# A half-rotary embedding on one core: the store of tile 1 waits for a subtraction instead of the multiplication ahead of it

## The chip, the cores and the metric

The kernel runs on one core of one Trainium2 chip. The metric is the device time of one execution in microseconds (us); lower is better. Of the kernel before three executions were timed, and one more was recorded by the hardware profiler.

## The reference

The input `x` has the shape (16, 512, 16, 64): batch, sequence, heads and the 64 elements of a head, in float32. `cos` and `sin` have the shape (512, 32), of which the first 16 columns are used. Cut to what matters:

```python
x1, x2 = x[..., :32], x[..., 32:]
c, s = cos[None, :, None, :16], sin[None, :, None, :16]
first  = x1[..., :16] * c - x1[..., 16:] * s
second = x1[..., :16] * s + x1[..., 16:] * c
out = concatenate([first, second, x2], axis=-1)
```

Half of each head is rotated and the other half is copied. 33.55 MB are read and as many are written.

## The kernel before, in words

**Tiles.** The input is cut into four tiles (0 to 3). A tile has 128 partitions with 16 sequence rows (`K = 16`) of 16 heads of 64 elements each, 64 KB in each partition and 8.4 MB in all. The tile `ring` in SBUF has three slots, and tile t lies in slot t mod 3. So tile 3 is loaded into the slot of tile 0, and that load has to wait until tile 0 has been stored. A slot holds its tile as it was loaded and is overwritten in place by the rotated half; a store writes the whole slot, both halves.

**Tables.** `cos` and `sin` are loaded once on GpSimd's queue (L64, L65), and VectorE spreads them over the 128 partitions (L74 to L84). This happens at the start and has no part in the change.

**The rotation.** All arithmetic is VectorE's, in the function `rotate`, which takes a tile and a range of its rows and issues four instructions: a multiplication by the sine into a scratch tile `b_t` in PSUM (L97), a multiplication by the cosine in place (L98), a subtraction on the first 16 columns (L99), and an addition on the next 16 (L106). `rotate` returns two things: one instruction, and the list `done` of its additions. The first of the two is used for one thing alone, the variable `near`, from the call for rows 0 to 4 of tile 2 (`KM = 5`).

**The order of the work.** The order on each queue is the order in which the program is written. VectorE rotates tile 0 (rows 0 to 7, then 8 to 15), tile 1 (likewise), tile 2 (rows 8 to 15, then 0 to 4, then 5 to 7), and tile 3 (rows 0 to 7, then 8 to 15). SyncE's queue issues the loads of tile 0, of tile 1 and of rows 8 to 15 of tile 2, the two halves of the store of tile 0, the load of rows 0 to 7 of tile 2, the load of tile 3, and the store of tile 3. GpSimd's queue issues the loads of the tables, the store of tile 1 and the store of tile 2.

**The hold.** Tile 1 is rotated long before its store is issued. The function `hold` makes a transfer wait for one more instruction, and the store of tile 1 (`behind_loads`) is held in this way until `near`; the reason that the code gives is that the store is to follow the loads at the DMA engines. Behind it on GpSimd's queue stands the store of tile 2, which waits for the last addition of tile 2.

Of the kernel before, what the change touches and what calls it, by code (L numbers as in the profile page):

```python
# [1 line left out]

# [4 lines left out]


@with_exitstack
def kernel(  # L10
    ctx: ExitStack,
    tc: tile.TileContext,
    x: bass.AP,
    cos: bass.AP,
    sin: bass.AP,
    out: bass.AP,
):
    nc = tc.nc
    fp32 = mybir.dt.float32
    P = 128  # L20
    B, S, H, D = x.shape
    Q = D // 4
    HF = D // 2

    K = 16
    T = B * S // (P * K)
    PB = S // K
    REP = P // PB  # L30
    R = H * D
    NS = 3
    KC = K // 2
    KM = 5
    KP = K - 4

    xf = x.rearrange("b s h d -> (b s h d)").rearrange("(t p f) -> t p f", t=T, p=P)
    of = out.rearrange("b s h d -> (b s h d)").rearrange("(t p f) -> t p f", t=T, p=P)
    cosf = cos.rearrange("(p k) j -> p (k j)", k=K)
    sinf = sin.rearrange("(p k) j -> p (k j)", k=K)  # L40

    const_pool = ctx.enter_context(tc.tile_pool(name="const", bufs=1))
    b_pool = ctx.enter_context(tc.tile_pool(name="bp", bufs=1, space=bass.MemoryType.PSUM))


    ring = const_pool.tile([P, NS, K, H, D], fp32)
    stage = const_pool.tile([P, 2, K, HF], fp32)
    spun = const_pool.tile([P, 2 * K, Q], fp32)
    packed = const_pool.tile([PB, 2 * K, Q], fp32)
    table = const_pool.tile([P, 2, K, 2, Q], fp32)  # L50

    def rows(t, lo, hi):
        return ring[:, t % NS, lo:hi].rearrange("p k h d -> p (k h d)")

    def load(t, lo=0, hi=K):
        return nc.sync.dma_start(out=rows(t, lo, hi), in_=xf[t, :, lo * R : hi * R])

    def store(t, lo=0, hi=K, queue=nc.sync):
        return queue.dma_start(out=of[t, :, lo * R : hi * R], in_=rows(t, lo, hi))  # L59


    nc.vector.memset(stage[:, :, :, 0:Q], 0.0)  # L62
    spread = stage.rearrange("(j b) t k i -> j b t (k i)", b=REP)
    nc.gpsimd.dma_start(out=spread[:, 0, 0], in_=cosf)  # L64
    nc.gpsimd.dma_start(out=spread[:, 0, 1], in_=sinf)  # L65
    load(0)
    load(1)
    load(2, KC, K)

    PQ = PB // REP
    nc.vector.stream_shuffle(  # L74
        out=spun[:],
        in_=stage.rearrange("p t k j -> p (t k) j")[:, :, 0:Q],
        mask=[j % PQ * REP for j in range(PB)],
    )
    for q in reversed(range(REP)):
        n = PQ * (q + 1)  # L80
        nc.vector.tensor_copy(out=packed[0:n], in_=spun[q * PB : q * PB + n])  # L81

    for r in range(REP):
        nc.vector.tensor_copy(  # L84
            out=table[r * PB : (r + 1) * PB].rearrange("p t k c j -> p (t k) c j"),
            in_=packed.unsqueeze(2).to_broadcast((PB, 2 * K, 2, Q)),
        )
    C = table[:, 0].rearrange("p k c j -> p k (c j)")
    Sn = table[:, 1].rearrange("p k c j -> p k (c j)")

    def rotate(t, lo, hi, cut=None):
        x1 = ring[:, t % NS, lo:hi, :, 0:HF]
        c = C[:, lo:hi].unsqueeze(2).to_broadcast((P, hi - lo, H, HF))
        s = Sn[:, lo:hi].unsqueeze(2).to_broadcast((P, hi - lo, H, HF))
        b_full = b_pool.tile([P, KC, H, HF], fp32, name="b_t")
        b_t = b_full[:, 0 : hi - lo]
        nc.vector.tensor_mul(out=b_t, in0=x1, in1=s)  # L97
        scaled = nc.vector.tensor_mul(out=x1, in0=x1, in1=c)  # L98
        nc.vector.tensor_sub(  # L99
            out=x1[:, :, :, 0:Q], in0=x1[:, :, :, 0:Q], in1=b_t[:, :, :, Q:HF]  # L100
        )
        ends = [hi - lo] if cut is None else [cut - lo, hi - lo]
        done = []
        for a, b in zip([0] + ends, ends):
            done.append(
                nc.vector.tensor_add(  # L106
                    out=x1[:, a:b, :, Q:HF],
                    in0=x1[:, a:b, :, Q:HF],
                    in1=b_t[:, a:b, :, 0:Q],
                )  # L110
            )
        return scaled, done

    def hold(transfer, point):
        tc.add_manual_dep(
            transfer.ins,
            point.ins.name,
            mybir.DependencyInfo(
                mybir.DependencyClass.Sync, mybir.DependencyReason.DATA
            ),  # L120
            reason="the store follows the loads at the DMA engines",
        )

    rotate(0, 0, KC)
    _, close = rotate(0, KC, K, cut=KP)
    hold(store(0, 0, KC), close[0])
    store(0, KC, K)
    load(2, 0, KC)
    load(3)
    rotate(1, 0, KC)  # L130
    rotate(1, KC, K)
    behind_loads = store(1, queue=nc.gpsimd)
    rotate(2, KC, K)
    near, _ = rotate(2, 0, KM)
    rotate(2, KM, KC)
    store(2, queue=nc.gpsimd)

    hold(behind_loads, near)
    rotate(3, 0, KC)
    rotate(3, KC, K)  # L140
    store(3)


# [1 line left out]
_INS = ['x', 'cos', 'sin']  # L145
_OUTS = [((16, 512, 16, 64), 'float32')]


# [23 lines left out]
```

## Time and profile before

| | us |
|---|---|
| median of three timed executions (161.75 to 162.19) | 161.84 |
| the profiled execution | 162.47 |
| its span, from the first to the last instruction | 160.7 |
| VectorE busy (70% of the span) | 113.0 |
| GpSimd busy (2% of the span) | 2.5 |

Data moved at 419 GB/s over the span, and 67.24 MB passed in all. TensorE and ScalarE do no work. The profile comes from one execution, and its times count from the first instruction. 1.8 us of the profiled execution lie outside its span, and that execution was 0.6 us longer than the median of the timed ones. "Issue" of a DMA is the instruction that starts it on a queue; the data move later, on the 16 DMA engines that all queues share. In a table by stretches of time, the DMA share counts each packet wholly in the stretch in which it begins, so that in a short stretch the share can be above 1.

### The profile page before, as it was taken

What the parts mean: (1) busy time and instruction counts of PE and PEld (TensorE: products, weight loads), DVE (VectorE), ACT (ScalarE), POOL (GpSimd) and SP (SyncE); (2) the same over time, 40 slices, a digit from 0 to 9 for tenths busy, and PEclk for the clock granted to TensorE, in tenths of its full rate; (3) what the DMA queues carried; (4) which work ended last, traced back from release to release, by engine and by line L of the source; (5) the groups of instructions that cost most, each with busy time, mean ns of one, the idle gap of its engine ahead of it and who ended that gap; (6) DMA issues with size and microseconds to landing.
All of it is one profiled execution on the core that took longest, in us unless ns stands there. A gap on an engine that the chain in (4) does not pass through costs nothing.

```text
span 160.7 us, 120 instructions
## 1 busy us (share of the span) xinstructions
DVE 113.0 (70%) x48; POOL 2.5 (2%) x8
## 2 busy tenths in 40 slices
DVE  1000959999999999999999999999999970000000
POOL 3000000000000000000000001010000000000000
DMA  7969969969899999999999699699799799799790
GB/s 261 522 277 538 490 294 522 490 294 522 375 408 392 473 432 400 465 441 400 408 506 522 277 506 490 294 490 506 310 490 506 310 490 473 343 490 473 343 490 33
DMA packets 1504, 67.24 MB, mean 419 GB/s; under 512 B 192, under 2 KB 192, under 8 KB 224
## 3 DMA queue, kind: packets, MB, share of 16 engines
q1 hardware_dynamic: 1152, 50.33, 73.1%
q0 software_dynamic: 352, 16.91, 24.3%
HBM read 33.69 MB, written 33.55 MB: 419 GB/s over the span
## 4 chain that ended last, share of the span: by engine, by line
DVE 62%; DMA 14%; issue 5%; DVEq 1%
DVE b_t L97 22%; DVE ring L98 22%; DMA ring<-in_x_dram 14%; DVE ring L106 10%; DVE ring L99 7%; DVEq L167 1%; DVEq L97 0%
## 5 line engine op out<-in xcount | busy, mean ns | idle before, releaser
L97 DVE TENSOR_TENSOR b_t<-ring,table 128x4096 f32<-128x4096 f32 (+2 forms) x9 | 35.6, 3959 | 2.1 <-DMA ring<-in_x_dram 1.9
L98 DVE TENSOR_TENSOR ring<-ring,table 128x4096 f32<-128x4096 f32 (+2 forms) x9 | 35.6, 3950 | 0.3
L99 DVE TENSOR_TENSOR ring<-ring,b_t 128x2048 f32<-128x2048 f32 (+2 forms) x9 | 18.4, 2050 | 0.3
L106 DVE TENSOR_TENSOR ring<-ring,b_t 128x2048 f32<-128x2048 f32 (+3 forms) x10 | 18.4, 1853 | 0.0
L74 DVE LOAD_MASK_SELECT spun<-stage x1 | 0.0, 14 | 14.6 <-DMA stage<-in_sin_dram 14.6
L84 DVE COPY table<-packed 32x1024 f32<-32x1024 f32 x4 | 2.7, 684 | 0.1
L59 POOL DMA_DIRECT2D out_dram<-ring x2 | 1.1, 550 | 101.4 <-DVE ring L98 93.6
L81 DVE COPY packed<-spun 32x512 f32<-32x512 f32 (+3 forms) x4 | 1.7, 416 | 0.1
L62 DVE MEMSET stage<- 128x512 f32 x1 | 0.5, 485 | 0.9 <-PEq L156 0.9
L74 DVE STREAM_SHUFFLE spun<-stage 128x512 f32<-128x512 f32 x1 | 0.7, 723 | 0.0
L64 POOL DMA_DIRECT2D stage<-in_cos_dram x1 | 0.6, 642 | 1.3 <-DVE stage L62 1.3
L65 POOL DMA_DIRECT2D stage<-in_sin_dram x1 | 0.5, 545 | 0.0
L156 POOL MEMSET const-float32-0.0<- 128x1 f32 x1 | 0.1, 98 | 0.2 <-issue 0.2
L156 POOL MEMSET const-bfloat16-1.0<- 128x1 bf16 x1 | 0.1, 101 | 0.0
L156 POOL MEMSET const-float32-1.0<- 128x1 f32 x1 | 0.1, 98 | 0.0
L156 POOL MEMSET const-uint8-127<- 128x1 uint8 x1 | 0.1, 98 | 0.0
## 6 DMA issues: line engine op xcount, KB each, us to landing
ring<-in_x_dram SPq DMA_DIRECT2D x2, 4096.0 KB, 40.7
out_dram<-ring SPq DMA_DIRECT2D x2, 4096.0 KB, 17.3
stage<-in_cos_dram POOLq DMA_DIRECT2D x1, 64.0 KB, 9.2
stage<-in_sin_dram POOLq DMA_DIRECT2D x1, 64.0 KB, 13.6
ring<-in_x_dram SPq DMA_DIRECT2D x3, 32.3
out_dram<-ring POOLq DMA_DIRECT2D x2, 33.7
out_dram<-ring SPq DMA_DIRECT2D x1, 28.2
```

What stands on the lines that cost most here:

```text
L59: return queue.dma_start(out=of[t, :, lo * R : hi * R], in_=rows(t, lo, hi))
L62: nc.vector.memset(stage[:, :, :, 0:Q], 0.0)
L64: nc.gpsimd.dma_start(out=spread[:, 0, 0], in_=cosf)
L65: nc.gpsimd.dma_start(out=spread[:, 0, 1], in_=sinf)
L74: nc.vector.stream_shuffle(out=spun[:], in_=stage.rearrange("p t k j -> p (t k) j")[:, :, 0:Q], mask=[j % PQ * REP for j in range(PB)],)
L81: nc.vector.tensor_copy(out=packed[0:n], in_=spun[q * PB : q * PB + n])
L84: nc.vector.tensor_copy(out=table[r * PB : (r + 1) * PB].rearrange("p t k c j -> p (t k) c j"), in_=packed.unsqueeze(2).to_broadcast((PB, ...
L97: nc.vector.tensor_mul(out=b_t, in0=x1, in1=s)
L98: scaled = nc.vector.tensor_mul(out=x1, in0=x1, in1=c)
L99: nc.vector.tensor_sub(out=x1[:, :, :, 0:Q], in0=x1[:, :, :, 0:Q], in1=b_t[:, :, :, Q:HF])
L106: nc.vector.tensor_add(out=x1[:, a:b, :, Q:HF], in0=x1[:, a:b, :, Q:HF], in1=b_t[:, a:b, :, 0:Q],)
L167: with _tile.TileContext(nc) as tc:
```

## The change

`rotate` returns its subtraction (L99) in place of its second multiplication (L98). Since only `near` uses that value, one thing follows: the store of tile 1 on GpSimd's queue waits for the subtraction of rows 0 to 4 of tile 2 instead of the multiplication ahead of it. No instruction is added or taken away, and the order on every engine and queue is the same.

```diff
         nc.vector.tensor_mul(out=b_t, in0=x1, in1=s)
-        scaled = nc.vector.tensor_mul(out=x1, in0=x1, in1=c)
-        nc.vector.tensor_sub(
+        nc.vector.tensor_mul(out=x1, in0=x1, in1=c)
+        first = nc.vector.tensor_sub(
             out=x1[:, :, :, 0:Q], in0=x1[:, :, :, 0:Q], in1=b_t[:, :, :, Q:HF]
         )
...
-        return scaled, done
+        return first, done
```

## The prediction, made before the changed kernel had run

> **What bounds the kernel now.** I first read the page's line of DMA shares and the chain that ended last.
>
> ```profile
> DVE  1000959999999999999999999999999970000000
> DMA  7969969969899999999999699699799799799790
> ...
> DVE 62%; DMA 14%; issue 5%; DVEq 1%
> ```
>
> The chain names VectorE (DVE) for 62% of the span. But VectorE is done at 131.5 us and the transfers go on for almost 28 us more, while the DMA row is full from the first slices to the last. The dips to 6 and 7 are an artefact of counting: a packet belongs to the slice in which it begins. So I take the 16 DMA engines as the bound: 67.24 MB at 419 GB/s are 160.5 us, the whole span. A change counts here only if it makes DMA engines idle or slow.
>
> Next, the timeline around the held store (POOL is GpSimd).
>
> ```profile
> 93.41 2.82 DVE L98 TENSOR_TENSOR ring<-ring,table 128x2560 f32<-128x2560 f32 x1
> 96.27 1.49 DVE L99 TENSOR_TENSOR ring<-ring,b_t 128x1280 f32<-128x1280 f32 x1
> 96.53 0.56 POOL L59 DMA_DIRECT2D out_dram<-ring  x1 [93.64 <-DVE ring L98]
> 97.67 1.48 DVE L106 TENSOR_TENSOR ring<-ring,b_t 128x1280 f32<-128x1280 f32 x1
> 99.19 1.77 DVE L97 TENSOR_TENSOR b_t<-ring,table 128x1536 f32<-128x1536 f32 x1
> ...
> 104.89 0.54 POOL L59 DMA_DIRECT2D out_dram<-ring  x1 [7.80 <-DVE ring L106]
> ```
>
> Columns: start, duration, instruction. The multiplication ends at about 96.24, and GpSimd issues the store of tile 1 at 96.53, 0.29 us later. The subtraction ends at 96.27 + 1.49 = 97.76.
>
> Last, the busy time by stretches. I laid each so that every one of the 16 engines begins exactly one data packet in it; share times width is then the mean duration of a packet.
>
> ```profile
> core 0: us, DVE busy (x) POOL busy (x), PEclk, DMA share, GB/s
> 1.70:2.60 0.90, 0.00 (x0) 0.90 (x2) 1.00 3.44 1165
> 4.70:5.60 0.90, 0.00 (x0) 0.00 (x0) 1.00 2.69 1165
> ...
> 49.85:50.65 0.80, 0.77 (x2) 0.00 (x0) 1.00 1.52 655
> 94.70:95.60 0.90, 0.90 (x1) 0.00 (x0) 1.00 2.69 1165
> 97.10:98.00 0.90, 0.90 (x2) 0.00 (x0) 1.00 3.05 1165
> ```
>
> A 64 KB packet takes 2.69 x 0.90 = 2.42 us in steady state (94.70). The last packets of the load of tile 3, which begin at 97.10 to 98.00, take 3.05 x 0.90 = 2.74 us: the hand-over to the store of tile 1 costs an engine 0.32 us on average. The first packets of the program (1.70), begun on cold engines, take 3.44 x 0.90 = 3.10 us, 0.68 too many. The hand-over from loads to the first store on SyncE's queue (49.85, packets of 32 KB) takes 1.52 x 0.80 = 1.22 us, against 1.21 in steady state, so next to nothing.
>
> The trace's records of single packets give the rest. The last load packets begin at 97.19 to 97.89 on the 16 engines and would end at 99.61 to 100.31 at the steady 2.42 us. They end at 99.84 to 101.46, and the store's first packets follow at once. From there to the end every engine has a packet, so what one loses here it ends late by. The engine that ends last (159.42) is the one that lost most, 1.15 us. It is also the only one that took a store packet before the load's closing signal.
>
> **The change, part by part.**
>
> 1. The trigger moves from the end of the multiplication to the end of the subtraction. The issue comes at 97.76 + 0.29 = about 98.04 instead of 96.53: 1.5 us later. One instruction of 1.49 us by its own row; nothing on VectorE is added. In the built program the subtraction raises a signal of its own and GpSimd's wait counts to it (before, it shared the addition's signal, at 99.16).
>
> 2. What stands behind it on GpSimd's queue is the store of tile 2, which waits until 104.61. GpSimd is free again at 98.04 + 0.56 = 98.60, so this costs nothing. Nobody on VectorE or SyncE waits for the store of tile 1 before the end: its slot isn't used again. SyncE's queue passes nothing new.
>
> 3. The later store at the DMA engines is the open point. At its own pace the first engine needs the store at 99.61, the last at 100.31. How long after the issue is a store ready for the engines? The lower bound is the first load of the program on SyncE's queue: issue at 0.74, first packet at 1.75, so 1.01 us. That makes 99.05, before any engine is free: no loss. On the last engine the store stood ready when its load packet began, at 97.89 (it went ahead of the signal), and on those that began up to 97.63 it did not: 1.1 to 1.4 us, by which 98.04 becomes 99.1 to 99.4, again early enough. The upper bound is what happened before: issue 96.53, first store packet 99.84, 3.31 us. That makes 101.35, and the engines would idle up to 1.5 us, the whole shift.
>
> 4. Ready is not yet hidden. An engine chooses its next packet about one packet ahead: the store of tile 3, issued at 131.51, was passed over by an engine that began a new packet at 134.60 and taken by one that did at 135.03, 3.1 to 3.5 us after its issue, against 1.01 on idle engines. The lead, from ready to the end of the last load packet, was about 2 us before. It becomes 0.2 to 1.2 us. The hand-over at 49.85 had a lead of 1.0 to 1.7 us (ready at 49.07 + 1.01, packets ending at 51.11 to 51.79) and cost nothing, so a lead of 1.0 is enough on that queue; most engines will have less. A cold start costs 0.68 by the row at 1.70, and no lead at all up to 1.5 by point 3. I take 0.6 us beyond today's loss, nearest to the cold start, and keep 0 and 1.5 as ends. Below nothing is possible too; see the second rival.
>
> 5. The pages bear on point 3. A row: GpSimd's issue at 96.53 under the subtraction took 0.56 us, the one at 104.89 under a multiplication with two operands in SBUF took 0.54, so VectorE didn't hold up GpSimd. The Trainium skill, SBUF — State Buffer, section "SBUF: two separate sides", says that GpSimd, which writes the descriptors of its own DMAs, is locked out by a VectorE instruction in a two-port mode until that ends. By that rule descriptors not written by 99.19, when the next multiplication begins, would wait until it ends at 100.96, and the change would cost about 1.4 us, as an estimate; no run here shows such a lock, and the two rows speak against it.
>
> The sum, on the profiled execution: span 160.7 + 0.6 = 161.3, with the 1.8 us outside it 163.1. That execution was 0.63 above the median, so against the median 161.84 + 0.6 = 162.45.
>
> **The rivals.**
>
> Nothing changes: the store is ready at 99.1 to 99.4, every engine finds it when its load packet ends, and the hand-over loses what it did. For it: points 1 to 3 taken with the 1.1 to 1.4 us, and that the latest engine, which sets the end, keeps the longest lead, 0.9 to 1.2 us. Against it: the hand-over at 97 already lost 0.32 where SyncE's at 50 lost nothing, so GpSimd's queue is less smooth than the 1.01 says. Time: 161.85, within 0.45.
>
> Faster: the stretched packets are the price of the store coming up while load packets are under way. Before, it comes up as those packets begin, and they lose 0.32 on average and 1.15 on the engine that ends last. If it comes up only in their last 0.2 to 1.2 us, or if the load's closing signal goes first everywhere, that engine gets its loss back. The most is 1.15, less what the others lose: those end by 159.18, 158.75 and 158.31, so if the two worst are cured the end comes 0.67 earlier, and with the third 1.1. The median execution had 0.6 us less to cure than the profiled one, so I price it at 0.75: 161.1. It decides if the cost depends on the overlap and if the lead of 0.2 to 1.2 us is enough.
>
> The wait is not the one the change says: were the subtraction still to share the addition's signal, the store would come at 99.45, 2.9 us later, the engines would idle at least 0.1 us by the 1.01 and up to 2.9, and the time would be near 163.3. The built program speaks against it; it is in the chance of slower.
>
> **How the numbers follow.** 0.3%, about 0.5 us, is what a measurement of this kernel can tell from no change. Slower by the short lead: 0.40, at 162.45; its own range is 162.35 to 163.3 (161.84 + 0.5 to 1.5). Unchanged: 0.28. Faster: 0.32, from 160.7 to 161.35. No case holds half, so the range must take in most of all three: from 160.95, which leaves out about a third of the faster case, to 163.1, which leaves out the upper part of the slower one.
>
> **What would show it.** In the changed trace the wait on GpSimd names L99, and the issue is at about 98.0. The stretch of the last load packets, opened at 97.10, shows the mean packet: above 2.74 us, or store packets that begin after a gap or take more than 2.42, if I am right; 2.74 if nothing changes; near 2.42, with the load landing by 100.7 on all engines, if the faster rival is. All transfers should end 0.6 us later than at 159.42, with VectorE unchanged. I am wrong if the packets run on without loss though the issue is at 98.0: then the lead doesn't matter.

## The result and the profile after

| | before | after |
|---|---|---|
| median of 13 timed executions, us | 162.19 (161.62 to 162.59) | 162.57 (162.39 to 162.92) |
| profiled execution, us | 162.47 | 162.59 |
| its span, us | 160.7 | 160.7 |
| last transfer ends, us (packet records) | 159.42 | 159.48 |

The ratio of after to before is 1.0026 (95% interval 1.0014 to 1.0039): a loss of 0.26%, or 0.4 us, just inside the 0.3% of the prediction. The kernel before was timed again beside the changed one; over 13 executions its median is 162.19, above the 161.84 of the three shown at first. The times after lie closer together than those before: they span 0.53 us against 0.97.

The wait moved as the change says. These are the waits on GpSimd and the timeline of the changed kernel:

```profile
POOL out_dram L59 <- DVE ring L99: 94.9, 1, 94.9
POOL out_dram L59 <- DVE ring L106: 6.3, 1, 6.3
```

```profile
95.97 1.49 DVE L99 TENSOR_TENSOR ring<-ring,b_t 128x1280 f32<-128x1280 f32 x1
97.37 1.48 DVE L106 TENSOR_TENSOR ring<-ring,b_t 128x1280 f32<-128x1280 f32 x1
97.75 0.56 POOL L59 DMA_DIRECT2D out_dram<-ring  x1 [94.86 <-DVE ring L99]
```

The issue comes 0.29 us after the subtraction's end (95.97 + 1.49). In this execution all of VectorE's work lies 0.3 us earlier than in the profile of before, so the issue shows at 97.75 and not at 98.04. The store of tile 2 waits 6.3 us instead of 7.8 behind it, and is issued as before when tile 2 is done.

The busy time by stretches of the changed kernel. The DMA share is the column before the GB/s, and a packet counts where it begins. In the stretches at 97.10, 99.60 and 103.40 each of the 16 DMA engines begins one data packet:

```profile
core 0: us, DVE busy (x) POOL busy (x), PEclk, DMA share, GB/s
...
97.10:98.00 0.90, 0.90 (x2) 0.24 (x1) 1.00 2.69 1165
99.60:100.20 0.60, 0.60 (x1) 0.00 (x0) 1.00 6.29 1748
102.00:103.30 1.30, 1.26 (x2) 0.00 (x0) 1.00 0.00 0
103.40:104.00 0.60, 0.60 (x2) 0.00 (x0) 1.00 4.03 1748
```

And the first packets of the store of tile 1 in the kernel before, 1.47 x 1.70 = 2.50 us:

```profile
99.80:101.50 1.70, 1.67 (x2) 0.00 (x0) 1.00 1.47 617
```

In the stretch at 102.00 none of the 16 engines begins anything. The last load packets (97.10) take 2.69 x 0.90 = 2.42 us, the steady duration: their stretch, 2.74 before, is gone. But the first packets of the store of tile 1 (99.60) take 6.29 x 0.60 = 3.77 us in place of 2.42, and the second ones (103.40) are again at 4.03 x 0.60 = 2.42. So the hand-over from loads to stores, which lost 0.39 us per engine before (0.32 in load packets and 0.07 in the store's), now loses 1.35, all in the store's first packets.

That the time rose by 0.4 us only, while the mean loss rose by 0.96, is a matter of which engine ends last. Before, the engine that ended last lost 1.15 us, one that was well ahead of it 1.61, and the others 0 to 0.75; after, all lose 1.2 to 1.5. The mean of the 16 engines' ends went from 158.22 to 159.18, the last from 159.42 to 159.48.

### The profile page after: what moved, and what is told of

Same layout as the page of the kernel before. It is cut to its first block, busy times and chain, and to the rows that moved or that the text cites. A ratio compares the mean times of both kernels' runs of the same rounds, so it can differ in the third digit from the quotient of the medians.

```text
span 160.7 us, 120 instructions
## 1 busy us (share of the span) xinstructions
DVE 113.0 (70%) x48; POOL 2.5 (2%) x8
## 4 chain that ended last, share of the span: by engine, by line
DVE 61%; DMA 14%; issue 5%; DVEq 1%
DVE b_t L97 22%; DVE ring L98 22%; DMA ring<-in_x_dram 14%; DVE ring L106 10%; DVE ring L99 7%; DVEq L167 1%; DVEq L97 0%
## 5 line engine op out<-in xcount | busy, mean ns | idle before, releaser
L98 DVE TENSOR_TENSOR ring<-ring,table 128x4096 f32<-128x4096 f32 (+2 forms) x9 | 35.6, 3950 | 0.3
L99 DVE TENSOR_TENSOR ring<-ring,b_t 128x2048 f32<-128x2048 f32 (+2 forms) x9 | 18.4, 2049 | 0.3
L59 POOL DMA_DIRECT2D out_dram<-ring x2 | 1.1, 552 | 101.1 <-DVE ring L99 94.9
```

The lines of the kernel that those rows point to most:

```text
L99: first = nc.vector.tensor_sub(out=x1[:, :, :, 0:Q], in0=x1[:, :, :, 0:Q], in1=b_t[:, :, :, Q:HF])
```

## The experiments

All edits are against the changed kernel unless another is named. Whether a store is "ready" no record shows; the text takes it to be ready as long after its issue as the first packet came on engines that had nothing to do: 1.13 to 1.28 us on GpSimd's queue (e2) and 0.85 to 0.96 on SyncE's (e8). "Loss" is what the trace's packet records show per engine at the hand-over, against 2.42 us a packet and no pause, as a mean over the 16 engines. Ratios are to the kernel before, timed alongside (median 162.24 for the first four, 162.17 for the next four).

| run | queue, wait | issue | loss, and where | last transfer ends | median, ratio (95%) |
|---|---|---|---|---|---|
| e1 | GpSimd, first multiplication | 93.50 | 0.64, load packets | 159.21 | 162.22, 1.0003 (0.9989 to 1.0018) |
| before | GpSimd, second multiplication | 96.53 | 0.39, mostly load packets | 159.42 | |
| e9, before again | GpSimd, second multiplication | 96.30 | 0.59, load packets | 159.21 | one time, 162.28 |
| after | GpSimd, subtraction | 97.75 | 1.35, store packets | 159.48 | 162.57, 1.0026 (1.0014 to 1.0039) |
| e10, after again | GpSimd, subtraction | 98.09 | 1.37, store packets | 159.64 | one time, 162.75 |
| e6 | GpSimd, multiplication of rows 0 to 6 | 98.47 | 1.18, store packets | 159.44 | 162.57, 1.0023 (1.0013 to 1.0033) |
| e2 | GpSimd, addition | 99.28 | 0.62, pause | 158.76 | 161.85, 0.9976 (0.9966 to 0.9987) |
| e4 | SyncE, its data alone | 76.94 | 0.55, load packets | 158.98 | 162.45, 1.0004 (0.9991 to 1.0017) |
| e7 | SyncE, second multiplication | 96.03 | 0.65, load packets | 158.78 | 162.34, 1.0012 (0.9998 to 1.0026) |
| e3 | SyncE, subtraction | 97.62 | 0.01 | 158.24 | 161.60, 0.9960 (0.9945 to 0.9976) |
| e8 | SyncE, addition | 98.98 | 0.06, pause | 158.19 | 161.66, 0.9961 (0.9947 to 0.9975) |
| e5 | ScalarE, subtraction | 97.71 | 0.79, store packets | 159.19 | 162.29, 1.0001 (0.9986 to 1.0015) |
| e12 | ScalarE, addition | 98.98 | 0.24, pause and store packets | 158.82 | one time, 162.08 |
| e11 | GpSimd, subtraction, row 0 stored early | 97.95 | 0.04, load packets | 159.00 | one time, 162.07 |

### First round: when and where the store is issued

The changed trace suggested Theory A: from 97.75 to the true start of data (103.5 less 2.42, so 101.1) are 3.35 us, the delay that the upper bound of the prediction had named. Theory B was a fixed price of the turn.

e1:

```diff
-        nc.vector.tensor_mul(out=b_t, in0=x1, in1=s)
+        first = nc.vector.tensor_mul(out=b_t, in0=x1, in1=s)
...
-        first = nc.vector.tensor_sub(
+        nc.vector.tensor_sub(
```

> The store of tile 1 waits for the sine multiplication of rows 0 to 4 (L97), which ends at 93.38 us, so its issue on GpSimd's queue comes at 93.4 to 93.7, 2.8 us earlier than before the change. Theory A (GpSimd's queue needs about 3.35 us from the issue to the first data, and an engine that runs out of load packets earlier than that stands idle): data at 96.8 to 97.0, ahead of the last load packets, so no packet is stretched by more than 0.1 us on average, some engines take a store packet before their last load packet, and the time is 1.0 us below that of before: ratio 0.994 (0.992 to 0.996). Theory B (turning from loads to a store of GpSimd's queue costs an engine 0.3 to 1.4 us each time, whenever it is issued): the stretch stays, on other packets, mean at least 0.3 us, and the time is within 0.3% of before.

Measured: no gain. The stretches of e1 that hold the load packets in flight when the store came up, and the two rounds of packets behind them:

```profile
94.80:95.70 0.90, 0.90 (x1) 0.00 (x0) 1.00 3.40 1165
97.60:98.90 1.30, 1.30 (x1) 0.00 (x0) 1.00 1.86 807
100.05:101.30 1.25, 1.22 (x2) 0.00 (x0) 1.00 1.93 839
```

3.40 x 0.90 = 3.06 us: the load packets ahead of the first store packet are stretched by 0.64, as Theory B has it. Then the engines take store, load and store packets in turn, and each round is at 1.86 x 1.30 = 2.42 and 1.93 x 1.25 = 2.41 us. So in this overlap only the first turn costs, and not the alternation of loads and stores.

e2:

```diff
-    near, _ = rotate(2, 0, KM)
+    _, ends = rotate(2, 0, KM)
+    near = ends[0]
```

> The store waits for the addition of rows 0 to 4, which ends about 1.4 us after the subtraction, so the issue comes at 99.1 to 99.4. Theory A (3.35 us from issue to data, engines idle until then): the first store packets end at about 99.15 + 3.35 + 2.42 = 104.9, 1.4 us later than in the changed kernel on every engine, and the time rises by the whole 1.4 us: 164.0, ratio to before 1.011 (1.009 to 1.013). Theory B (a fixed cost of a cold start of 1.2 to 1.5 us, the store being ready 1.1 to 1.4 us after its issue): the engines are free at 99.6 to 100.1 and the store is ready at 100.2 to 100.5, so only about 0.4 us is added: 162.95, ratio 1.005.

Measured: faster than both kernels, against either theory. Timeline and stretches of e2:

```profile
99.01 1.77 DVE L97 TENSOR_TENSOR b_t<-ring,table 128x1536 f32<-128x1536 f32 x1
99.28 0.56 POOL L59 DMA_DIRECT2D out_dram<-ring  x1 [96.39 <-DVE ring L106]
```

```profile
99.60:100.40 0.80, 0.80 (x1) 0.24 (x1) 1.00 0.01 0
100.40:100.60 0.20, 0.20 (x1) 0.00 (x0) 1.00 12.31 5243
```

The engines run dry and nothing begins until 100.40 (the 0.01 are closing signals); then all 16 begin within 0.2 us, 100.41 to 100.56 by the records, with packets of 12.31 x 0.20 = 2.46 us. That is 1.13 to 1.28 us after the issue, not 3.35: Theory A is out, and so is a cold start of 0.7 us or more after such a pause. Issued 1.5 us later than in the changed kernel, the store ends its first packets earlier (102.9 to 103.0 against 103.4 to 103.9). The mean loss, 0.62, is above that of the kernel before, but the pause is longest for the engine that was free first (at least 0.78, from 99.63 to 100.41) and shortest for the last (at most 0.28, from 100.29): it levels the engines, and the ends lie at 158.64 to 158.76.

e3:

```diff
-    behind_loads = store(1, queue=nc.gpsimd)
+    behind_loads = store(1)
```

> The store of tile 1 waits for the same subtraction as in the changed kernel, but is issued on SyncE's queue, behind the load of tile 3. Theory A (the 3.35 us belong to GpSimd's queue; SyncE's needs about 1.0): issue at 97.8 to 98.1, ready at 98.8 to 99.1, before any engine is free at 99.6; stretch at the hand-over at most 0.1 us on average, time 1.0 us below that of before: ratio 0.994 (0.992 to 0.997). Theory B (a lead of less than 1 us leaves the engines cold on any queue): first store packets stretched by 0.7 us or more, time like the changed kernel's, ratio 1.000 to 1.003.

Measured: no loss, as Theory A foresaw for another reason; the gain is 0.4% rather than 0.6%. Theory B's fixed price doesn't hold on this queue. The issue in e3, and its stretches, last load packets and first store packets:

```profile
97.62 0.34 SPq L59 DMA_DIRECT2D out_dram<-ring  x1
```

```profile
97.20:97.85 0.65, 0.65 (x2) 0.00 (x0) 1.00 3.73 1613
99.60:100.35 0.75, 0.75 (x1) 0.00 (x0) 1.00 3.24 1398
```

3.73 x 0.65 = 2.42 and 3.24 x 0.75 = 2.43 us. This is the fastest of the versions, level with e8.

e4, the same with the hold taken out:

```diff
-    behind_loads = store(1, queue=nc.gpsimd)
+    behind_loads = store(1)
...
-    hold(behind_loads, near)
```

> The store of tile 1 is issued on SyncE's queue behind the load of tile 3 and held for nothing but its own data (done at 77.1); being in the same queue it follows the load at the engines anyway. Both theories: no stretch at the hand-over, all engines full to the end, time 1.0 to 1.2 us below that of before: ratio 0.993 (0.991 to 0.996). If instead the hand-over is stretched here too, by 0.3 us or more, the cost belongs to the turn from loads to stores at this point of the program and neither theory holds.

Measured: a miss for both. The last load packets, which end before the store in the same queue begins, are stretched to 4.94 x 0.60 = 2.96 us:

```profile
97.25:97.85 0.60, 0.60 (x2) 0.00 (x0) 1.00 4.94 1748
```

So by the last sentence of the expectation neither theory held. A store that stands ready early costs about 0.6 us in the load packet ahead of it (0.55 here, 0.64 in e1), on either queue.

### Second round: queue and time of arrival apart

e5 and e6:

```diff
-    behind_loads = store(1, queue=nc.gpsimd)
+    behind_loads = store(1, queue=nc.scalar)
```

> The first four runs felled both theories: the store held till the addition (issue 99.28) put data on the engines 1.13 to 1.28 us after its issue, earlier than in the changed kernel, and lost only the idle gap (0.62 us per engine on average), while the changed kernel's first store packets are stretched by 1.35 us on every engine; on SyncE's queue with the same wait nothing was lost. Here the store waits for the subtraction and is issued on ScalarE's queue, a second queue like GpSimd's but started in the way of SyncE's. Theory C (taking the turn from one queue to another while the last load packet is under way costs about 1.3 us): the first store packets are stretched by 1.0 us or more, time like the changed kernel's, ratio to before 1.001 to 1.004. Theory D (the cost comes with GpSimd's queue alone): hand-over loss at most 0.2 us per engine, time like that of SyncE's queue with this wait, ratio 0.996 (0.994 to 0.998).

e6, against the kernel before:

```diff
-    KM = 5
+    KM = 7
```

> The kernel before with KM = 7: the store waits for the cosine multiplication again, but that of rows 0 to 6, which ends at about 98.1. The issue on GpSimd's queue falls at 98.35, between that of the changed kernel (97.75) and that of the wait for the addition (99.28), and the store is ready at 99.5 to 99.65 by the 1.13 to 1.28 us of the latter, 0 to 0.6 us before the engines come free (99.6 to 100.1). Theory C and D alike leave open where the cost ends. If it is paid by any store that comes up before an engine has run out of load packets: stretch of 1.0 us or more on most engines, data from 101 on, ratio 1.002 to 1.005. If it falls with the time that the store overlaps the last load packet: loss of at most 0.4 us per engine, the best of the waits on GpSimd's queue, ratio 0.995 to 0.998.

Measured, the first store packets of e5, then of e6:

```profile
99.60:100.60 1.00, 1.00 (x1) 0.00 (x0) 1.00 3.21 1049
```

```profile
99.65:100.15 0.50, 0.50 (x2) 0.00 (x0) 1.00 7.17 2097
```

ScalarE's queue gives 3.21 us, 0.79 too many, between the two theories: more than SyncE's queue with the same wait, less than GpSimd's. In e6 the mean is 7.17 x 0.50 = 3.59. It is not one value: 14 engines took the store straight behind the load's signal and needed 3.48 to 3.97, while the two that had paused, by 0.07 to 0.24 us, needed 2.72 and 2.81. Those two were through at 102.7 and 102.9, their neighbours at 103.2 to 103.9. So on GpSimd's queue the price is paid in the first store packet even when the store comes up only shortly before the engine is dry, and most of it falls away once the engine has paused.

e7, against the kernel before, and e8, against e2:

```diff
-    behind_loads = store(1, queue=nc.gpsimd)
+    behind_loads = store(1)
```

> The store waits for the cosine multiplication of rows 0 to 4 as before the change, on SyncE's queue. Issue at 96.2, ready 1.0 us later at 97.2, when the engines begin their last load packets (97.2 to 97.9). With the subtraction's wait (ready 98.6) nothing was lost on this queue, with no hold at all (ready long ago) 0.55 us in the last load packets. Theory E (an engine that knows its next packet, a store, when it begins the last load packet pays 0.2 to 1.0 us in that packet): loss between, 0.2 to 0.6 us per engine, mostly on engines that began after 97.2, ratio 0.997 to 1.000. If the queue alone matters and not the time: as with the subtraction's wait, loss under 0.1, ratio 0.996.

> The store waits for the addition, on SyncE's queue. Issue at 99.1, ready 1.0 us later at 100.1 to 100.15; the engines are free at 99.6 to 100.1, so that they idle 0.3 us on average and the latest of them not at all; the packets after the gap are no longer than 2.47 us. Loss 0.2 to 0.5 us per engine on average, ratio to before 0.997 to 0.999, between that of the subtraction's wait on this queue (0.996) and that of the addition's wait on GpSimd's (0.9976) or near them. A loss above 0.8 us would say that SyncE's queue too has a bad time of arrival and that GpSimd's is not special.

Measured: e7's last load packets take 6.14 x 0.50 = 3.07 us, a loss of 0.65, just above what Theory E allowed; all engines pay, and the ratio is a little above its range. In e8 the loss is 0.06, below what I expected, since the store was ready 0.85 to 0.96 us after its issue rather than 1.0 or later. Last load packets of e7, first store packets of e8 (4.09 x 0.60 = 2.45 us):

```profile
97.30:97.80 0.50, 0.50 (x2) 0.00 (x0) 1.00 6.14 2097
```

```profile
99.70:100.30 0.60, 0.60 (x1) 0.00 (x0) 1.00 4.09 1748
```

### Third round: the two kernels again, and two looks at the cause

> The kernel before, unchanged, profiled a second time. Its times spread over 161.6 to 162.6, the changed kernel's over 162.4 to 162.9. If the spread comes from the hand-over, the loss there differs from that of the first profile (0.39 us per engine on average, 1.15 on the engine that ended last), while all other stretches of the DMA engines lose the same; the hand-over's mean stays at 0.2 to 0.7, below the changed kernel's 1.35, and the last transfers end at 158.3 to 159.4.

> The changed kernel, unchanged, profiled a second time. The loss in the first store packets is there again on every engine, 1.2 to 1.5 us, with unstretched load packets ahead of it, and the last transfers end within 0.2 us of 159.5. If the 1.35 us were an accident of one execution, the loss would be nearer to that of the kernel before, 0.4.

Both kernels unchanged. Last load packets of the kernel before (3.35 x 0.90 = 3.02 us), and first store packets of the changed one (4.47 x 0.85 = 3.80 us):

```profile
97.10:98.00 0.90, 0.90 (x2) 0.00 (x0) 1.00 3.35 1165
```

```profile
99.50:100.35 0.85, 0.85 (x1) 0.00 (x0) 1.00 4.47 1234
```

The stretch after is no accident. The kernel before has a loss that varies: 0.39 and 0.59 on average, and 1.15 and 1.14 in the worst load packet. Between this pair of profiles the last transfer moves by 0.43 us, between the first pair by 0.06; the medians say 0.38.

One part of e9's expectation fails: the other stretches do not all lose the same. At the first turn from loads to a store, on SyncE's queue at about 50 us, a packet takes 1.19 x 1.10 = 1.31 us in e9, against 1.22 in the first profile of the kernel before:

```profile
49.60:50.70 1.10, 1.07 (x2) 0.00 (x0) 1.00 1.19 477
```

Over all the profiles this turn costs 0 to 0.2 us per engine, most in e7 (1.41 us a packet), though no edit touches the work up to there.

e11:

```diff
-    behind_loads = store(1, queue=nc.gpsimd)
+    store(1, 0, 1, queue=nc.gpsimd)
+    behind_loads = store(1, 1, K, queue=nc.gpsimd)
```

> The changed kernel with row 0 of tile 1 stored on GpSimd's queue as soon as it is rotated (issue at about 64), and the other 15 rows as the change has it. Theory F (GpSimd's queue is cold after 80 us without work, and its first packet pays): the queue has worked until about 75, so the hand-over at 99.6 loses at most 0.4 us per engine. Theory G (turning from loads to a store of another queue is what costs, if the engine has no pause): the first packets of the 15 rows (60 KB, steady 2.27 us) are stretched by 1.1 to 1.5 us as in the changed kernel.

Measured: a loss of 0.04, within Theory F's bound and against Theory G's 1.1 to 1.5. Its last load packets and the first packets of the 15 rows, 2.24 x 1.10 = 2.46 and 1.90 x 1.20 = 2.28 us:

```profile
98.60:99.70 1.10, 1.07 (x2) 0.00 (x0) 1.00 2.24 953
101.10:102.30 1.20, 1.20 (x1) 0.00 (x0) 1.00 1.90 819
```

But the row stored early pushed the loads back, so that they ended at 101.2 to 102.3 and not at 99.6 to 100.1, and the store, issued at 97.95, was ready at 99.1 to 99.2, 2 to 3 us ahead of the engines instead of 0.6 to 1.2. It must be compared with the kernel before, which with such a lead lost 0.39 and 0.59. That leans to Theory F, and doesn't settle it.

The traces of e3, e4, e5 and e7 speak against Theory F in its plain form. In these runs the store of tile 2 is GpSimd's first DMA since the tables, whose data were through by 13.1 us. It is issued at about 104.7, when the engines are taking store packets from another queue. In e4 every engine begins its first packet of that store in the second of these stretches:

```profile
107.20:108.30 1.10, 1.10 (x1) 0.00 (x0) 1.00 2.20 953
109.60:110.70 1.10, 1.10 (x1) 0.00 (x0) 1.00 2.20 953
```

2.20 x 1.10 = 2.42 us, the steady duration, ahead of the turn and in it; in all four runs no packet that begins from 103 to 114 takes longer. So neither a queue that has been without work for over 90 us nor a change of queue costs anything by itself. If either matters at 99.6, it does so together with the turn from loads to a store.

e12 (one time, 162.08, beside 162.33 for the kernel before), against e2:

```diff
-    behind_loads = store(1, queue=nc.gpsimd)
+    behind_loads = store(1, queue=nc.scalar)
```

> The store waits for the addition, on ScalarE's queue. Issue at 99.0 to 99.1; ready 1.0 us later, after most engines have run out of load packets. Theory G (only an engine that goes straight from a load packet to a store of another queue pays; one that has paused doesn't): engines with a pause lose the pause alone, first packets at most 2.5 us, mean loss below 0.5 us, against 0.78 with the subtraction's wait on the same queue, and any engine without a pause shows a first packet of 3.0 us or more. If a second queue always costs: 0.8 us in the first packets whether they pause or not.

Measured, the first store packets:

```profile
99.60:100.35 0.75, 0.75 (x1) 0.00 (x0) 1.00 3.46 1398
```

3.46 x 0.75 = 2.60 us on average, against 3.21 with the subtraction's wait: a later issue is cheaper on this queue too, and the mean loss of 0.24 is as Theory G said. Its condition on single engines is not borne out: of the engines whose store packet begins straight behind the load packet one needed 3.24 us, but no other packet took more than 2.82, under the 3.0 that it asked.

## Why the prediction was right, and where it was not

The direction was right and the time, 162.57, is near the forecast 162.45; the change of 0.38 us is under the 0.61 forecast, and lies within the 0.3% that I had called "same". That the time came so near is partly luck: the forecast started from 161.84, and the kernel before measured 162.19 over 13 executions. The base was 0.35 us too low and the change 0.23 too high, and the two errors partly cancel. By steps:

1. The trigger (point 1): right. The issue follows the subtraction by 0.29 us, at 97.75 and 98.09 in two profiles against 98.04 forecast, and VectorE is unchanged.

2. What stands behind it (point 2): right, nothing was late.

3. Ready at the engines (point 3): of its three figures (1.01, 1.1 to 1.4, 3.31) the 1.1 to 1.4 us read off the last engine was right; e2 measured 1.13 to 1.28. The 3.31 us were no delay of the queue at all.

4. The lead (point 4): this step failed, in its reason and in its size. I argued that the price grows as the lead shrinks, up to a cold start of 0.68 us and more. In e2 the lead is below nothing, and the first packets take 2.46 us; on SyncE's queue a lead of 1.1 to 1.8 us costs nothing (e3) and one of nearly 3 us or more costs 0.55 to 0.65 (e7, e4). What costs most on GpSimd's queue is a store that comes up in the last 1.2 us or so of an engine's last load packet (after, e10, e6: 1.18 to 1.37); earlier it costs a third to a half of that, in the load packet (before, e9, e1), and once the engine is dry only the pause (e2). One support of the step was a single profile: that the hand-over at 49.85 cost nothing is so there, but in other profiles this turn costs up to 0.2 us.

   Taken as a term of the sum, "0.6 us beyond today's loss" measured 0.96 on the mean engine in the first pair of profiles and 0.78 in the second, but 0.06 and 0.43 at the end, because the engine that ends last had already paid 1.15 us before. I had noted that engine and still put a mean into the sum, and my sign that all transfers end 0.6 us later did not come in that form: the mean end moved by 0.96, the last by 0.06. I had also called it the one that lost most: in a single packet that is so, but another lost 1.61 us over two packets and ended earlier (159.18) because it had been ahead.

5. The page (point 5): by the Trainium skill's SBUF — State Buffer, section "SBUF: two separate sides", GpSimd can't write descriptors while VectorE runs an instruction in a two-port mode. My estimate of 1.4 us took the multiplication at 99.19 to be such an instruction, and no row gave a reason for that. In e2 the store is issued at 99.28 under a multiplication with both inputs in SBUF, which runs to 100.78, and data begin from 100.41. This multiplication did not lock GpSimd out, and no run here shows such a lock; the two rows told right.

The rival "nothing changes" had the time nearly right and the trace wrong. The rival "faster" foresaw half of what happened: the load packets are back at 2.42 us and the load's closing signal goes first on every engine, but the loss came back, larger, in the store's first packets. That the wait was not the one named is refuted by the L99 in the waits.

What is shown: when and on which queue the store comes up sets the loss at the hand-over, and the time follows the engine that comes through it last. In e3, the kernel before and the changed kernel the loss is 0.01, 0.39 and 1.35 us, and the engines end at 157.85, 158.22 and 159.18 on average. What stays open: what an engine does in the 1.35 us. e11 points to a queue that has been without work, e5 and e12 to the change of queue; the store of tile 2 shows that neither costs anything among stores, and no run tells them apart cleanly at the turn from loads. Nor was it tried whether smaller packets at the end of the load shrink the price.

## What to carry to other kernels

Where the DMA engines set the end, look at the last turn from loads to stores, and at the engine that comes last out of it, not only at the mean: a later trigger that makes all engines begin together can end earlier than one that leaves one straggler. A wait that is tuned for when a transfer comes up should be tried on both sides, for the price isn't monotone in the delay (here, against the kernel before, +0.26% for a wait 1.5 us later and -0.24% for one 2.9 us later). And a store that only has to follow a load is worth trying in the load's own queue, held until less than about 2 us before the engines run out: that was worth 0.4% here, with a lead of 1.1 to 1.8 us (e3) and of 0.4 or none (e8), and with no hold it was worth nothing (e4).

## What the runs showed that I had not expected

- A store of GpSimd's queue that comes up 0.2 to 1.2 us before the engines run out of load packets has first packets of 3.77 and 3.80 us (2.42 steady). With the same wait they take 3.21 on ScalarE's queue, and 2.43 on SyncE's, that of the loads. One that comes up when the engines are dry takes 2.46.
- A store that stands ready when a load packet begins, or comes up in its first 0.6 us, stretches that load packet: 2.74 to 3.07 us on average (before, e9, e1, e4, e7), on GpSimd's queue and on the load's own. The exception is e11, with 2.46.
- From the issue to the first packet on dry engines: 1.13 to 1.28 us on GpSimd's queue (e2), 0.85 to 0.96 on SyncE's (e8).
